# Inverses' transfers behind the queries' rotation, the substitution behind the keys', and modulation steps in the attention

## The chip, the core and the metric

The kernel runs on one core of a Trainium2 chip. The metric is the device time of one execution in microseconds (us); it is measured in several runs and the median is given. Engines: TensorE (PE), VectorE (DVE), ScalarE (ACT), GpSimd (POOL) and SyncE (SP), which here only issues DMAs.

## The reference

Two networks of two layers each follow one another on an activation x of 256 tokens by 1024 features, in float32.

A layer of the first is `x = norm(a*x + hybrid_mixer(x))`, then the same with a cross-attention to a memory, then with an MLP, `square(relu(x @ w_up)) @ w_down`. The hybrid mixer runs three attentions on one projection: a sparse one (compressed, selected and window branches), a latent one and one with forget gates.

A layer of the second is

```python
mod = c_act @ w_ada + b_ada                  # c_act = silu(c), 1024 x 3072
shift, scale, gate = split(mod)
h = rms_norm_2(x, norm_g) * (1.0 + scale) + shift
# h @ w_in is split into a pool branch, a retention (q, k, v, gate) and an RWKV-7 branch
qh = rotary(q); kh = rotary(k) * dh ** -0.5  # 4 heads of 128; rotate-half with cos, sin
# RWKV-7, for each token: S = S * w + (S a) b + v k;  y = S r
x = x + gate * (merged @ w_out)
```

The modulation `mod` depends on c alone, so its product with w_ada (24 pieces of 512 KB a layer) can be made anywhere ahead of the second network.

## The kernel before

**Products and weights.** Every float32 product is three TensorE products of split operands (`mm3`, L138 to L140). A weight unit of 512 KB is loaded by SP in program order (`fetch`) into one of four `raw` buffers; ACT casts it to `hi` (L112), DVE subtracts to get `lo` (L113); each has six slots. `gemm_b` makes a tile of 128 features by 256 tokens, `gemm_a` of 128 tokens by 512 features. A tile scheduler places the instructions of DVE, ACT and POOL; PE's order is written out by hand in the attention and in the second network.

**Side jobs.** `fillers` is a list of small jobs that `fill(n)` takes from. For each of the first network's layers it holds first a set-up job (`clear_scratch`, which writes zeros to two DRAM scratch arrays `zd` and `lt`, or the three `trig_steps` that make `cos` and `sin`), then the 24 modulation steps of one layer of the second network (`ada_steps`). A step loads a piece of w_ada into a `raw` buffer and lets DVE multiply it by c and reduce (L1641, one instruction and a read of the accumulator). `fill` is called in the MLP alone: one job after each pair of tiles of `up` for g of 1 and more (L929), and two, two and four jobs in `down` (L939); `fill(99)` empties the list at the end of the layer.

**Attention of the first network.** The loop at L730 goes through a list of slots. Each slot advances one or two of the jobs (m0, m1: latent; c0, c1: compressed; 00 to 11: selected and window; f0, f1: forgetting) and one piece of the dense products that run beside them (`dense`). The softmax steps are DVE's (L275 and on), the transposes go through one `t` buffer in PSUM, which DVE copies out (L315, L627 is a transpose of the compressed branch).

**Rotation and substitution in the second network.** RWKV-7's recurrence is solved in chunks, and the chunks' triangular matrices are inverted from blocks of 16. `masked` writes the matrices to the scratch `lt`, `band` reads their diagonal blocks back, and 15 rounds of a product and a sum on DVE (L1518, L1519: the substitution) invert all the blocks at once. The result goes through POOL's queue to `zd` (L1520), and four transfers, also on POOL's queue, read it back in another layout as `TT` (`inverse_parts`, L1195). `invert` (L1202) reads TT later. Beside it `rotated` (L1372 and on) makes the keys (chunk 4) and then the queries (chunk 3): four tiles each, and for each tile two ACT copies into a `row` buffer (three such buffers), a POOL product with sin (L1384), a DVE product with cos (L1386) and a POOL sum into `gt` (L1387). Behind the queries PE does the first half of a gate (`silu_gate`, two of four tiles), the retention's scores (L1398) and its state products (L1403).

## Time and profile before

| what | value |
|---|---|
| median of 3 runs | 1619.14 us (1618.19 to 1619.34) |
| the profiled execution's own time | 1620.32 us |
| its span in the profile | 1618.5 us |
| mean granted PE clock | 0.978 |
| PE busy | 1554.8 us, 96% |
| PE weight load busy | 1432.2 us, 88% |
| DVE, ACT, POOL busy | 1100.4, 744.8, 261.1 us |
| DMA moved | 288.98 MB, 179 GB/s on average |

Busy times are sums over an engine's instructions. The span is the profile's time from first to last instruction. A bracket behind a row of a timeline, `[2.79 <-POOL gt L1387]`, is the time that the engine stood idle before it, and whose result it waited for. The granted clock is 1.00 at 2.4 GHz and 0.50 at 1.2 GHz.

### The profile page before, as it was taken

The page shows a single profiled execution, that of the slowest core. Times are in us where ns is not written, and L with a number is a line of the kernel's source. Part 1 is how long each engine was busy: PE and PEld are TensorE (multiplying, and loading weights), DVE is VectorE, ACT ScalarE, POOL GpSimd, SP SyncE. Part 2 cuts the span into 40 slices and gives each one's busy share as a digit, 9 for nine tenths or more (in the row PEclk, how much of TensorE's full clock was granted, in tenths as well). Part 3 has the DMA queues.
Part 4 walks back from the last instruction along what each step waited for, and adds up shares of the span by engine and source line. Part 5 has one row for each costly group of instructions (what it writes and reads, how often), then busy time and mean ns, then how long its engine had stood idle before and what let it go on. Part 6 is the DMA issues. An engine that isn't in the chain of part 4 may idle for free. (4 is left out here: it accounts for less than half of the span.)

```text
span 1618.5 us, 29835 instructions
## 1 busy us (share of the span) xinstructions
PE 1554.8 (96%) x12106; PEld 1432.2 (88%) x12106; DVE 1100.4 (68%) x1785; ACT 744.8 (46%) x1196; POOL 261.1 (16%) x255
## 2 busy tenths in 40 slices
PE   7999999999999999999999899899999998999998
PEld 6789997999878899988988788899999987999997
DVE  5576568767676766689776787666466775764754
ACT  4665444544445664455543374433444643333441
POOL 1000110101100001201111142401111433201202
PEclk9899999999999999999999989999999999999999
DMA  8733475587776234664777744543355435442451
GB/s 296 257 105 119 158 231 172 179 287 264 266 258 204 89 108 154 204 208 141 253 270 252 265 140 161 162 147 120 102 183 161 155 113 168 163 134 90 154 184 67
DMA packets 81033, 288.98 MB, mean 179 GB/s; under 512 B 9224, under 2 KB 10304, under 8 KB 80896
## 3 DMA queue, kind: packets, MB, share of 16 engines
q1 hardware_dynamic: 78768, 280.07, 51.9%
q0 software_dynamic: 2128, 7.01, 1.5%
q8 instruction: 95, 1.56, 0.4%
q14 instruction: 42, 0.34, 0.1%
HBM read 281.48 MB, written 5.55 MB: 177 GB/s over the span
## 5 line engine op out<-in xcount | busy, mean ns | idle before, releaser
L113 DVE TENSOR_TENSOR lo<-raw,hi 128x1024 fp32r<-128x1024 f32 (+1 forms) x429 | 543.3, 1275 | 227.3 <-ACT hi L112 224.6
L112 ACT CAST hi<-raw 128x1024 fp32r<-128x1024 f32 (+1 forms) x435 | 452.7, 1048 | 508.8 <-PE mm L139 220.9
L138 PE MATMUL mm<-act,hi 128*128 128x256 f32 x1744 | 506.1, 290 | 7.8 <-ACT hi L112 5.8
L140 PE MATMUL mm<-act,lo 128*128 128x256 f32 x1744 | 497.7, 285 | 3.2 <-DVE lo L113 3.2
L139 PE MATMUL mm<-act,hi 128*128 128x256 f32 x1744 | 497.0, 285 | 0.5 <-DVE act L128 0.5
L138 PEld LDWEIGHTS mm<-act,hi 128*128 128x128 f32 x1744 | 336.8, 193 | 15.8 <-ACT hi L112 6.2
L140 PEld LDWEIGHTS mm<-act,lo 128*128 128x128 f32 x1744 | 336.4, 193 | 5.4 <-DVE lo L113 3.9
L139 PEld LDWEIGHTS mm<-act,hi 128*128 128x128 f32 x1744 | 336.6, 193 | 2.0 <-DVE act L128 0.9
L138 PE MATMUL s<-act,hi 128*128 128x256 f32 x448 | 128.5, 287 | 5.5 <-ACT PT L921 5.5
L138 PE MATMUL mm<-hi,act 128*128 128x512 f32 (+1 forms) x320 | 125.2, 392 | 6.5 <-ACT hi L127 5.5
L140 PE MATMUL s<-act,lo 128*128 128x256 f32 x448 | 128.2, 286 | 0.0
L139 PE MATMUL s<-act,hi 128*128 128x256 f32 x448 | 128.2, 286 | 0.0
L139 PE MATMUL mm<-lo,act 128*128 128x512 f32 (+1 forms) x320 | 123.4, 386 | 0.9 <-DVE lo L113 0.9
L140 PE MATMUL mm<-hi,act 128*128 128x512 f32 (+1 forms) x320 | 123.2, 385 | 0.0
L138 PEld LDWEIGHTS s<-act,hi 128*128 128x128 f32 x448 | 87.4, 195 | 6.4 <-ACT PT L921 6.1
L139 PEld LDWEIGHTS s<-act,hi 128*128 128x128 f32 x448 | 87.3, 195 | 0.2
L140 PEld LDWEIGHTS s<-act,lo 128*128 128x128 f32 x448 | 87.5, 195 | 0.0
L1641 DVE CUSTOM_DVE_ANT_0 raw<-raw,gt 128x1024 f32<-128x1024 f32 x48 | 59.5, 1239 | 30.6 <-DMA raw<-in_w_ada 30.3
L138 PEld LDWEIGHTS mm<-hi,act 128*128 128x128 f32 x320 | 61.1, 191 | 19.6 <-ACT hi L127 5.5
L926 POOL TENSOR_TENSOR PT<-PT 128x512 f32<-128x512 f32 x28 | 38.5, 1376 | 236.3 <-ACT act L925 128.4
L138 PE MATMUL mm<-hi,P 128*128 128x512 f32 x192 | 74.8, 389 | 0.0
L139 PE MATMUL mm<-lo,P 128*128 128x512 f32 x192 | 74.8, 389 | 0.0
(519 smaller groups left out, 2439.8 us busy)
## 6 DMA issues: line engine op xcount, KB each, us to landing
raw<-in_w_in SPq DMA_DIRECT2D x119, 512.0 KB, 4.4
raw<-in_w_up SPq DMA_DIRECT2D x64, 512.0 KB, 4.5
raw<-in_w_down SPq DMA_DIRECT2D x64, 512.0 KB, 4.7
raw<-in_w_gate SPq DMA_DIRECT2D x48, 512.0 KB, 3.4
raw<-in_w_ada SPq DMA_DIRECT2D x48, 512.0 KB, 4.5
raw<-in_w_gl SPq DMA_DIRECT2D x48, 512.0 KB, 3.8
raw<-in_w_branch SPq DMA_DIRECT2D x24, 512.0 KB, 3.4
raw<-in_w_br SPq DMA_DIRECT2D x16, 512.0 KB, 3.3
```

The lines of the kernel that those rows point to most:

```text
L112: act.copy(out=h[:, :cols], in_=r[:, :cols])
L113: (eng or ver).tensor_sub(out=l[:, :cols], in0=r[:, :cols], in1=h.bitcast(F32)[:, :cols])
L138: pe.matmul(o, lhsT=lh, rhs=rh, start=first, stop=False)
L139: pe.matmul(o, lhsT=lh, rhs=rl, start=False, stop=False)
L140: pe.matmul(o, lhsT=ll, rhs=rh, start=False, stop=last)
L926: pool.tensor_mul(out=r, in0=r, in1=r)
L1641: ver.tensor_tensor_reduce(out=r, in0=r, in1=box["c"], scale=1.0, scalar=0.0, op0=ALU.mult, op1=ALU.add, accum_out=mods[l][:, o:o + 1])
```

## The change

Three things are changed.

*Second network.* The four TT transfers keep their place in the program on POOL's queue, which is behind all of the queries' rotation; before, the scheduler was free to place them. The substitution, and the zd transfer with it, is issued behind the last cosine product of the keys (`issue_after(last[0])`).

*Modulation.* c's activation is made once and kept in a tile of its own (`cmod`), where it was made once a layer in a `gt` buffer. The first ten steps of a layer come ahead of the set-up jobs in the list, and in the attention's slot loop every second slot takes one job as soon as more than three attention jobs have begun. `down` takes one job where it took two or four.

*Tiles.* Two tiles change their tag, from `flat` to `mv`.

```diff
--- before.py
+++ after.py
@@ -456,7 +456,7 @@
         pool.memset(rep, 0.0)
 
         def compress_hidden(i):
-            fl = bt("flat", [128, 16, 2, 16])
+            fl = bt("mv", [128, 16, 2, 16])
             pool.memset(fl[:, :, :, 15:16], 0.0)
             for g in range(2):
                 for par in range(2):
@@ -727,6 +727,7 @@
             job = {"m": attend_mla, "f": attend_fox, "c": attend_compressed}
             jobs = {}
             pieces = dense()
+            beside = 0
             for slot in ("m0", "c0", "m1", "m0 c0", "m0 00", "m1 c1", "m1 01", "00 c1", "00 f0", "01 10", "01 10", "f0",
                          "f0 f1", "10", "10", "10 11", "11", "f1", "f1", "11", "11", "11"):
                 for n in slot.split():
@@ -734,6 +735,10 @@
                         jobs[n] = job[n[0]](int(n[1])) if n[0] in job else attend_nsa(int(n[0]), int(n[1]))
                     next(jobs[n], None)
                 next(pieces, None)
+                if len(jobs) > 3:
+                    beside += 1
+                    if beside % 2 and beside < 20:
+                        fill(1)
             for _ in pieces:
                 pass
         x = xs[0]
@@ -936,7 +941,7 @@
                 us = [unit(T["w_down"][l, 16 * c + 4 * g + i]) for i in range(4)]
                 gemm_a([ys[0][c], ys[1][c]], op, us, first=g == 0, last=g == 3, t_outer=g == 3 and c == 1)
                 if g < 3:
-                    fill(2 if g < 2 else 4)
+                    fill(1)
                     continue
                 if c == 1:
                     nrm.params(l, 2)
@@ -1192,7 +1197,8 @@
 
             for n in range(2):
                 for a in range(2):
-                    pool.dma_start(out=TT[n][half(a)], in_=flat(K["zd"], 16 + 8 * HS * n + 64 * 129 * a, [128, 64], [HS, 8], [1, 64]))
+                    tc.keep_in_program_order(pool.dma_start(
+                        out=TT[n][half(a)], in_=flat(K["zd"], 16 + 8 * HS * n + 64 * 129 * a, [128, 64], [HS, 8], [1, 64])))
 
         def invert():
 
@@ -1369,6 +1375,8 @@
                 act.activation(out=gv, in_=p, func=AF.Tanh, scale=0.5)
                 ver.scalar_tensor_tensor(out=gv, in0=gv, scalar=1.0, in1=p, op0=ALU.add, op1=ALU.mult)
 
+        last = []
+
         def rotated(c):
             us = chunk_b(c)
             dst = bt("gt", [128, 4, 256])
@@ -1383,7 +1391,7 @@
                     act.copy(out=sw[64:128], in_=pi[0:64, :])
                     pool.tensor_mul(out=sw, in0=sw, in1=sin)
                     dv = dst[:, j + i, :]
-                    ver.tensor_mul(out=dv, in0=pi, in1=cos)
+                    last[:] = [ver.tensor_mul(out=dv, in0=pi, in1=cos).ins]
                     pool.tensor_add(out=dv, in0=dv, in1=sw)
             return dst
 
@@ -1505,19 +1513,20 @@
             bonus()
             rk_ = rotated(4)
             pool.tensor_mul(out=Ei, in0=Ei, in1=rT)
-            zb = bt("PT", [128, 31, 16])
-            pool.memset(zb, 0.0)
-            pool.memset(zb[:, 15:31, 0:1], 1.0)
-            tmp = bt("dg", [128, 256])
-            zrow = zb[:, 15:31, :]
-            for i in range(14, -1, -1):
-                m = 15 - i
-                zv = bass.AP(tensor=zrow.tensor, offset=zrow.offset + 16 * i + 15 + 1,
-                             ap=[list(zrow.ap[0]), [1, m], [15, m]])
-                tv = tmp[:, :m * m].rearrange("p (a b) -> p a b", b=m)
-                ver.tensor_mul(out=tv, in0=zv, in1=band[:, i, 1:m + 1].unsqueeze(1).broadcast_to([128, m, m]))
-                ver.reduce_sum(out=zrow[:, i, 1:m + 1], in_=tv, axis=AX.X)
-            pool.dma_start(out=flat(K["zd"], 16, *blocks), in_=zrow)
+            with tc.issue_after(last[0]):
+                zb = bt("PT", [128, 31, 16])
+                pool.memset(zb, 0.0)
+                pool.memset(zb[:, 15:31, 0:1], 1.0)
+                tmp = bt("dg", [128, 256])
+                zrow = zb[:, 15:31, :]
+                for i in range(14, -1, -1):
+                    m = 15 - i
+                    zv = bass.AP(tensor=zrow.tensor, offset=zrow.offset + 16 * i + 15 + 1,
+                                 ap=[list(zrow.ap[0]), [1, m], [15, m]])
+                    tv = tmp[:, :m * m].rearrange("p (a b) -> p a b", b=m)
+                    ver.tensor_mul(out=tv, in0=zv, in1=band[:, i, 1:m + 1].unsqueeze(1).broadcast_to([128, m, m]))
+                    ver.reduce_sum(out=zrow[:, i, 1:m + 1], in_=tv, axis=AX.X)
+                pool.dma_start(out=flat(K["zd"], 16, *blocks), in_=zrow)
             rq = rotated(3)
             dm = aux(T["ret_decay"]).rearrange("p (h t) -> p h t", t=256)
             inverse_parts()
@@ -1625,15 +1634,16 @@
                                          op0=ALU.mult, op1=ALU.mult)
                 fetch(out[128 * t:128 * t + 128, s], o)
 
+    box = {}
+
     def ada_steps(l):
 
-        box = {}
 
         def step(j, i):
             def f():
                 if not box:
                     r = raw_load(T["c"].partition_broadcast(128))
-                    c = box["c"] = bt("gt", [128, 1024])
+                    c = box["c"] = bt("cmod", [128, 1024])
                     act.activation(out=c, in_=r, func=AF.Tanh, scale=0.5)
                     ver.scalar_tensor_tensor(out=c, in0=c, scalar=1.0, in1=r, op0=ALU.add, op1=ALU.mult)
                 r = raw_load(T["w_ada"][l, j, i])
@@ -1654,7 +1664,7 @@
     scratch = {n: dr.tile([128 * 2080], F32, name=n) for n in ("zd", "lt")}
 
     def clear_scratch():
-        z = bt("flat", [128, 16, 2, 16]).rearrange("p a b c -> p (a b c)")[:, 0:416]
+        z = bt("mv", [128, 16, 2, 16]).rearrange("p a b c -> p (a b c)")[:, 0:416]
         pool.memset(z, 0.0)
         for d in scratch.values():
             pool.dma_start(out=flat(d, 0, [2080, 128], [416, 5], [1, 416]),
@@ -1708,7 +1718,8 @@
         blk[:] = b1, s1
         xop = new_op(8)
         for l in range(L):
-            fillers.extend((trig_steps() if l == 1 else [clear_scratch]) + ada_steps(l))
+            steps = ada_steps(l)
+            fillers.extend(steps[:10] + (trig_steps() if l == 1 else [clear_scratch]) + steps[10:])
             x, xop, us = block1_layer(l, x, xop, us, K1)
     r = xop
     fill(99)
```

**POOL, second network, layer 0.** The end of the keys' rotation and the queries' rotation; L1384 and L1387 are the sine product and the sum, `zd` the scratch, TT the tiles for the inverses. Before:

```order
L1387 TENSOR_TENSOR gt_10482<-gt_10482,row_10599 128x256
L1520 DMA zd<-PT_10606 2048x1x16
L1195 DMA TT_10355<-zd 64x8x64
L1384 TENSOR_TENSOR row_10715<-row_10715,sin 128x256
L1195 DMA TT_10355<-zd 64x8x64
L1387 TENSOR_TENSOR gt_10665<-gt_10665,row_10715 128x256
L1384 TENSOR_TENSOR row_10721<-row_10721,sin 128x256
L1195 DMA TT_10356<-zd 64x8x64
L1387 TENSOR_TENSOR gt_10665<-gt_10665,row_10721 128x256
L1195 DMA TT_10356<-zd 64x8x64
L1384 TENSOR_TENSOR row_10776<-row_10776,sin 128x256
L1387 TENSOR_TENSOR gt_10665<-gt_10665,row_10776 128x256
```

In the changed kernel the same lines are L1392, L1395, L1529 (zd) and L1200 (TT):

```order
L1395 TENSOR_TENSOR gt_10660<-gt_10660,row_10710 128x256
L1392 TENSOR_TENSOR row_10716<-row_10716,sin 128x256
L1395 TENSOR_TENSOR gt_10660<-gt_10660,row_10716 128x256
L1529 DMA zd<-PT_10601 2048x1x16
L1392 TENSOR_TENSOR row_10771<-row_10771,sin 128x256
L1395 TENSOR_TENSOR gt_10660<-gt_10660,row_10771 128x256
L1392 TENSOR_TENSOR row_10777<-row_10777,sin 128x256
L1395 TENSOR_TENSOR gt_10660<-gt_10660,row_10777 128x256
L1200 DMA TT_10350<-zd 64x8x64 x2
L1200 DMA TT_10351<-zd 64x8x64 x2
```

The zd transfer moved behind the queries' second sum, and all four TT transfers behind their fourth.

**DVE, at the same place.** L1518 and L1519 are the substitution's product and sum, L1386 the cosine product, L113 the weights' `lo` (`lo_10656` and `lo_10662` belong to the queries' weights, `lo_10798` is the first of the gate's). Before:

```order
L113 TENSOR_TENSOR lo_10656<-raw_10653,hi_10655 128x1024
L1518 TENSOR_TENSOR dg_10609<-PT_10606,dg_10353 128x49
L1519 TENSOR_REDUCE PT_10606<-dg_10609 128x7
L113 TENSOR_TENSOR lo_10662<-raw_10659,hi_10661 128x1024
L1386 TENSOR_TENSOR gt_10482<-mm_10483,cos 128x256
L1518 TENSOR_TENSOR dg_10609<-PT_10606,dg_10353 128x64
L1519 TENSOR_REDUCE PT_10606<-dg_10609 128x8
...
L1386 TENSOR_TENSOR gt_10482<-mm_10544,cos 128x256
L1519 TENSOR_REDUCE PT_10606<-dg_10609 128x15
L1386 TENSOR_TENSOR gt_10665<-mm_10666,cos 128x256 x2
L113 TENSOR_TENSOR lo_10798<-raw_10795,hi_10797 128x1024
```

In the changed kernel (L1527 and L1528 the substitution, L1394 the cosine product; `lo_10793` the first of the gate's):

```order
L113 TENSOR_TENSOR lo_10657<-raw_10654,hi_10656 128x1024
L1394 TENSOR_TENSOR gt_10477<-mm_10478,cos 128x256 x2
L1394 TENSOR_TENSOR gt_10477<-mm_10539,cos 128x256 x2
L1527 TENSOR_TENSOR dg_10604<-PT_10601,dg_10348 128x1
L1528 TENSOR_REDUCE PT_10601<-dg_10604 128x1
...
L1527 TENSOR_TENSOR dg_10604<-PT_10601,dg_10348 128x225
L1528 TENSOR_REDUCE PT_10601<-dg_10604 128x15
L113 TENSOR_TENSOR lo_10793<-raw_10790,hi_10792 128x1024
L1394 TENSOR_TENSOR gt_10660<-mm_10722,cos 128x256
L113 TENSOR_TENSOR lo_10799<-raw_10796,hi_10798 128x1024
```

The keys' four cosine products stand ahead of the whole substitution, and the gate's first `lo` directly behind its last sum.

**DVE, attention of layer 0**, the third modulation step of nine; L286 to L290 scale the softmax's rows, L315 copies a transpose out of `t`, L613 begins the compressed branch. Before:

```order
L286 RECIPROCAL sc_1085<-sums_873 128x4
L288 TENSOR_TENSOR sc_1085<-sc_1085,gate_631 128x4
L290 TENSOR_TENSOR P_871<-P_871,sc_1085 128x4x128
L315 COPY PT_962<-t_957 128x512
L613 TENSOR_TENSOR pcs_971<-s_972,bias_c 128x4x2x16
L286 RECIPROCAL sc_1089<-sums_874 128x4
```

In the changed kernel (the step is the two rows L1651):

```order
L286 RECIPROCAL sc_1096<-sums_873 128x4
L1651 ISA raw_1236,mod_76<-raw_1236,cmod_956 128x1024
L1651 ISA mod_76 128x1
L315 COPY PT_970<-t_965 128x512
L613 TENSOR_TENSOR pcs_979<-s_980,bias_c 128x4x2x16
L288 TENSOR_TENSOR sc_1096<-sc_1096,gate_631 128x4
L286 RECIPROCAL sc_1100<-sums_874 128x4
```

The step stands between the reciprocal and the copy of the transposes.

## Rows read from the trace of the kernel before

**Rows 1.** The page's first part: engine, busy us, share of the span, instructions.
```profile
PE 1554.8 (96%) x12106; PEld 1432.2 (88%) x12106; DVE 1100.4 (68%) x1785; ACT 744.8 (46%) x1196; POOL 261.1 (16%) x255
```

**Rows 2.** Busy time by window: stretch, length, five engines, granted clock, DMA share, GB/s.
```profile
60.00:180.00 120.00, 117.91 (x970) 107.11 (x970) 78.07 (x202) 74.57 (x178) 3.22 (x6) 1.00 0.40 134
300.00:525.00 225.00, 221.39 (x1449) 199.71 (x1448) 159.40 (x202) 109.26 (x147) 22.72 (x20) 0.99 0.77 257
760.00:921.00 161.00, 156.69 (x965) 141.46 (x964) 115.12 (x146) 76.78 (x88) 18.48 (x14) 0.99 0.78 263
1020.00:1052.00 32.00, 26.13 (x185) 24.68 (x184) 19.42 (x27) 12.23 (x19) 14.73 (x17) 0.89 0.46 127
1344.00:1384.00 40.00, 32.26 (x244) 31.40 (x244) 27.25 (x52) 15.23 (x26) 19.25 (x21) 0.87 0.46 141
```

**Rows 3.** Timeline of PE, block 2 layer 0: start, us, instruction, idle before and releaser.
```profile
1032.09 0.38 PE L138 MATMUL mm<-act,hi 128*128 128x256 f32 x1 [0.55 <-ACT hi L112]
...
1037.53 1.03 PE L1398 MATMUL mm<-gt,gt 128*128 128x256 f32 x4
1041.34 0.70 PE L1398 MATMUL mm<-gt,gt 128*128 128x256 f32 x2 [2.79 <-POOL gt L1387]
1043.82 1.22 PE L1398 MATMUL mm<-gt,gt 128*128 128x256 f32 x2 [1.77 <-POOL gt L1387]
```

**Rows 4.** Timeline of POOL, the same place.
```profile
1025.38 1.12 POOL L1520 DMA_DIRECT2D zd<-PT  x1
1032.80 0.71 POOL L1195 DMA_DIRECT2D TT<-zd  x1 [6.30 <-DMA zd<-PT]
```

**Rows 5.** Timeline of PE, block 2 layer 1.
```profile
1367.49 0.39 PE L140 MATMUL mm<-act,lo 128*128 128x256 f32 x1 [0.59 <-DVE lo L113]
...
1374.21 0.58 PE L138 MATMUL mm<-act,hi 128*128 128x256 f32 x1 [5.28 <-ACT hi L112]
...
1376.89 0.58 PE L140 MATMUL mm<-act,lo 128*128 128x256 f32 x1 [1.88 <-DVE lo L113]
...
1382.60 1.68 PE L1398 MATMUL mm<-gt,gt 128*128 128x256 f32 x7
```

**Rows 6.** Timeline of ACT, the same place.
```profile
1372.35 0.37 ACT L1382 COPY row<-mm 64x256 f32<-64x256 f32 x1 [6.17 <-POOL gt L1387]
```

**Rows 7.** Groups by line on DVE, whole kernel: count, busy us, mean ns, idle before.
```profile
L1518 DVE TENSOR_TENSOR dg<-PT,dg 128x1 f32<-128x1 f32 (+14 forms) x30 | 10.6, 352 | 3.6 <-DMA dg<-lt 2.8
...
L1519 DVE TENSOR_REDUCE PT<-dg 128x1 f32<-128x1 f32 (+14 forms) x30 | 7.1, 237 | 0.8
...
L1386 DVE TENSOR_TENSOR gt<-mm,cos 128x256 f32<-128x256 f32 x16 | 6.7, 419 | 15.5 <-ACT row L1383 15.5
```

**Rows 8.** The page's fifth part: two groups of DVE.
```profile
L113 DVE TENSOR_TENSOR lo<-raw,hi 128x1024 fp32r<-128x1024 f32 (+1 forms) x429 | 543.3, 1275 | 227.3 <-ACT hi L112 224.6
...
L1641 DVE CUSTOM_DVE_ANT_0 raw<-raw,gt 128x1024 f32<-128x1024 f32 x48 | 59.5, 1239 | 30.6 <-DMA raw<-in_w_ada 30.3
```

**Rows 9.** Busy time by window, three short stretches (columns as in rows 2).
```profile
421.00:426.00 5.00, 5.00 (x32) 5.00 (x31) 3.23 (x4) 2.51 (x4) 2.60 (x2) 0.66 0.48 166
828.00:830.00 2.00, 2.00 (x11) 2.00 (x11) 0.69 (x1) 1.78 (x2) 0.56 (x1) 0.50 0.91 330
1370.00:1380.00 10.00, 3.91 (x16) 3.62 (x17) 6.23 (x5) 5.45 (x8) 9.81 (x12) 0.51 0.45 138
```

**Rows 10.** Timeline of PE, the MLPs of layers 0 and 1.
```profile
419.90 0.39 PE L138 MATMUL s<-act,hi 128*128 128x256 f32 x1 [2.39 <-ACT PT L921]
...
826.84 0.39 PE L138 MATMUL s<-act,hi 128*128 128x256 f32 x1 [1.77 <-ACT PT L921]
```

**Rows 11.** Timeline of PE, the attention of layer 0.
```profile
107.90 0.33 PE L627 MATMUL t<-cpack,pcs 128*128 128x128 f32 x1 [1.19 <-DVE PT L315]
```

**Rows 12.** Timeline of POOL, block 2 layer 1.
```profile
1374.32 0.74 POOL L1387 TENSOR_TENSOR gt<-gt,row 128x256 f32<-128x256 f32 x1
...
1375.82 1.61 POOL L1387 TENSOR_TENSOR gt<-gt,row 128x256 f32<-128x256 f32 x1
```

## The prediction

> **What bounds the kernel now.** I read the engines' busy shares first. PE is busy for 1554.8 of 1618.5 us [rows 1], so the span is PE's work plus about 64 us in which it stands still, plus what the lower clock costs. An edit that touches none of PE's own matmuls can only win or lose there. So the table by stage comes next [rows 2]: its last three columns are PE's granted clock, the DMA share and the rate. Three kinds of place matter. In the attention of layer 0 PE loses 2.09 us of 120 (first row), with the DMA at 0.40, and layer 1 runs the same program. In the two MLPs it loses 3.61 and 4.31 us, with the DMA at 0.77 and 0.78. Around the keys' and queries' rotation of block 2 it loses 5.87 of 32 us and 7.74 of 40 us, and the clock falls to a mean of 0.89 and 0.87. Then I read the timelines there.
>
> In layer 0 of block 2 PE has finished the first half of the gate at 1037.5, does four score matmuls and waits 2.79 and 1.77 us for POOL's `gt` add [rows 3]. POOL is late because it issues the zd transfer at 1025.38 and then sits 6.30 us on its landing in front of the first TT transfer [rows 4]; the queries' sine products stand behind that TT. In layer 1 the same wait reaches PE another way: PE waits 0.59, 5.28 and 1.88 us in the gate [rows 5], since ACT's copy into `row` waited 6.17 us for POOL's add [rows 6] and the gate's casts stand behind that copy on ACT.
>
> **Part 1: TT and substitution in block 2.** After the change all four TTs stand behind the last query add on POOL, and the substitution stands behind the keys' last cosine product on DVE. Nothing new reads TT early: its readers, the inverses' transposes, stand over a hundred PE instructions behind the scores. So POOL's 6.30 us goes. What is late next is the gate's weights: their `lo` subtractions now stand behind the whole substitution on DVE.
>
> How long is that? A gate or rotation matmul costs 0.12 us (117.91 us for 970 [rows 2]). The gate of layer 0 starts about 12 matmuls ahead of 1032.09 less its 0.55 us wait [rows 3], near 1030.0; the queries' 96 matmuls take 11.5 us, so PE leaves the keys at 1018.5. Four ACT copies of 0.37 [rows 6] and two products of 0.42 [rows 7] later, at 1020.8, the substitution starts. It is 30 instructions, 10.6 and 7.1 us for both layers, so 8.9 us a layer [rows 7]; two cosine products of the queries (0.8) stand inside it, and I allow 1 us for the gaps between 30 dependent instructions, a tenth of their time, for which no row here stands: 10.7 us, to 1031.5. One subtraction of 1.28 [rows 8] later, at 1032.8, the gate's third matmul may go, which PE wanted at 1030.2: **a new wait of 2.6 us**. The second unit's subtraction, behind another product, adds 0.3; 34 more matmuls take 4.1, and the scores start at 1038.6, 1.1 later than before, but with their operands there. Gone are 2.79 + 1.77 = 4.6 us. The mean clock of 0.89 over 32 us is some 7 us at the half level; 4.6 of these were the waits, the other 2.4 us were matmuls that took twice their time (1.2 saved inside the window, about as much just after it). Layer 0: 4.6 + 2.4 - 1.1 = 5.9 us won.
>
> Layer 1: the gate's third matmul was wanted near 1366.8 (1367.49 less its wait of 0.59 [rows 5]). By the same steps the keys end at 1355.1, the substitution runs from 1357.4 to 1368.1, and the subtraction is done at 1369.4: again 2.6 us of wait. The scores start at 1369.4 + 1.2 + 0.3 + 4.1 = 1375.0 in place of 1382.60 [rows 5]: 7.6 us won. Together **13.5 us**.
>
> What can be given back is the clock. A wait of 2.39 us in the MLP was followed by a granted clock of 0.66 over 5 us, one of 1.77 us by the 1.2 GHz level (0.50) for the 2 us looked at [rows 9, 10]; the attention's wait of 1.19 us [rows 11] stands in a stage with a mean of 1.00 [rows 2]. Two new gaps of 2.6 us lie above both that fell. 5 us at 0.66 lose 1.7 us, so I take **3.4 us back** for the two: 10.1 us. Bounds: no new wait and no fall would win both windows' idle and slow time, 5.87 + 7.74 + 2.4 + 2 = 18 us (1370 to 1380 stood at 0.51 with 3.91 us busy, some 2 us too many [rows 9]); a substitution of twice my gaps and a clock that stays low as long as in layer 1 leave about 5.
>
> One cost speaks against the new order: POOL's products of the queries now run beside DVE's subtractions for the gate. Such a pairing shows before: a POOL add that takes 0.74 us takes 1.61 [rows 12]. Four at 1.61 behind a zd issue of 1.12 [rows 4] end at 1039.1, when the second half of the scores wants them, so I book nothing for it, and up to 1 us a layer in the range. The Trainium skill, page "SBUF — State Buffer", section "SBUF: two separate sides", says that VectorE and GpSimd hold a shared port pair as an exclusive lock, also when VectorE has two SBUF inputs. By that rule the substitution's products, with two SBUF inputs, would wait for POOL's rotation too, and the sum would be about 1 us a layer worse, by an estimate from the doubled add. The doubled add agrees with it; that the substitution is slowed, no row here settles.
>
> **Part 2: modulation steps.** A step is a 512 KB load into one of four `raw` buffers, a DVE product-and-reduce of 1.24 us [rows 8] and a short read. Ten come first in the list, the order shows nine a layer in the attention. They leave `down`; those in `up` stay.
>
> MLP, what it wins: both windows lose 3.61 + 4.31 us in waits [rows 2], and 1.7 and 1 us of slow matmuls behind the two waits named [rows 9, 10]: 10.6 us at most. DVE waits 30.6 us for the steps' loads in all [rows 8], so relief is plausible, but 15 of 24 steps stay, among them all that stand between `up`'s weights. I take 9/24 of 10.6: **4 us**; ends 0 and 10.6. The estimate is coarse: if the one late chain of 2.39 us goes with its slow matmuls, that is 4 us at once.
>
> Attention, what it costs: nine steps are 9 x 1.24 = 11 us of DVE a layer, on top of 78.07 busy in 120 [rows 2]; DVE has the room, but its softmax chain ends some waits of PE last, the `t` transpose at 107.90 among them [rows 11]. Ends: 0, if each step falls in DVE's idle time, and 2 x 11 = 22 us, if each lies on the path. PE's lost 2.09 us sit in few places, so I take two steps in nine as falling ahead of what PE waits for, 2.5 us a layer: **5 us lost**. On SP's queue the steps' loads stand ahead of later weights of the attention, which then wait for one more buffer; with the DMA at 0.40 [rows 2] I count that as 0. ACT gets c's activation there, whose table is the one that the softmax behind it needs: 0, beside ACT's idle third.
>
> **Part 3: the rest.** c is loaded, activated and multiplied once and not twice, which takes a cast-sized ACT and a DVE instruction off layer 1's MLP: 0, beside PE's work. The clear's two transfers leave the start of the kernel for layer 0's MLP, on POOL's queue in front of nothing that PE waits for: 0; without that cover, a few us at worst.
>
> **Sum.** -10.1 - 4 + 5 = -9.1. The profiled execution took 1620.32 us (span 1618.5), 1.2 above the runs' median of 1619.14; against the median the forecast is **1610.0 us**.
>
> **Rivals.**
> *The wait moves and little is left.* The gate's `lo` behind the substitution is later than I say, the clock falls at each gap and stays low as in layer 1 (0.51 for 10 us [rows 9]); block 2 wins 5, the MLP nothing: -5 + 5 = 0, about 1619; with half the attention's cost, 1616. For it: the new gap is as long as any outside block 2. Against: 5.28 us of layer 1's wait has no successor of that size.
> *Slower: the attention's chain on DVE decides.* From eleven or twelve of the eighteen steps on that lie ahead of what PE waits for, 14.1 / 1.24, the loss eats what block 2 and the MLP win; with all of them, 22 - 14 = +8, 1627, and more with the clock. For it: the softmax steps feed PE through `s` and `t` buffers that are few. Against: DVE is idle for a third of the stage.
> *Larger gain.* The gaps leave the clock up and the MLP's late chain goes whole: -13.5 - 10 + 3 = -20, about 1599.
> *The change doesn't do what it says in the MLP.* The steps that hurt are those in `up`, which stay: -10.1 + 5 = -5, 1614.
>
> **How the numbers follow.** Forecast case (1605 to 1613) 0.43; larger gain (1596 to 1605) 0.17; MLP unchanged (1613 to 1616) 0.19; little left (about 1616 to 1622) 0.09; slower by the attention 0.12. A measurement of this kernel tells a change from none at about 0.2%, 3.2 us. So faster 0.79, same 0.09, slower 0.12. The range is 1600 to 1618: it leaves out the slower case, part of the same, and the far end of the gain, about 0.2.
>
> **What would show it.** In block 2: no POOL idle before a TT; a PE wait on `lo` at the gate of 2 to 3 us a layer in place of the `gt` and `hi` waits; scores 5 to 8 us earlier after the stage's start; the clock at the half level or not behind the gap. In the MLP windows: idle below 3.6 and 4.3 us. In the attention windows: PE idle up by 1 to 5 us each, behind `t` or `s`. It is wrong if the attentions lose more than 10 us in all, or if the gate's wait exceeds 5 us.

## The result and the profile after

The changed kernel takes 1603.03 us (median of 4 runs, 1601.58 to 1606.92) beside 1619.24 us for the kernel before (1618.19 to 1622.14). The ratio is 0.9907, with an interval of 0.9883 to 0.9931: 11 to 19 us less. The forecast was 1610.0, in a range of 1600 to 1618. The profiled execution of the changed kernel is the longest of its four, 1606.92 us with a span of 1605.1.

The page's first part, against [rows 1]:

```profile
PE 1548.5 (96%) x12106; PEld 1427.4 (89%) x12106; DVE 1094.4 (68%) x1784; ACT 741.7 (46%) x1193; POOL 259.5 (16%) x255
```

PE is busy 6 us less, in a span that is 13 us shorter: slow matmuls went as well as waits. The same three windows as in [rows 2] (stretch, length, the five engines' busy time, granted clock, DMA share, GB/s):

```profile
60.00:180.00 120.00, 116.98 (x949) 104.98 (x948) 87.83 (x221) 74.63 (x179) 3.23 (x6) 0.99 0.51 169
300.00:525.00 225.00, 223.62 (x1473) 201.87 (x1471) 151.50 (x189) 111.80 (x148) 23.15 (x20) 1.00 0.73 243
760.00:921.00 161.00, 160.64 (x998) 145.31 (x997) 111.81 (x142) 75.97 (x92) 22.04 (x18) 1.00 0.71 239
```

The attention of layer 0 has 9.8 us more of DVE work (nine steps of 1.24 us are 11), and PE stands still for 3.02 us where it did for 2.09. The MLPs, which lost 3.61 and 4.31 us, lose 1.38 and 0.36, and their DMA share fell from 0.77 and 0.78 to 0.73 and 0.71. The whole list of PE's waits, three of its rows (engine, line, what was waited for: us in total, times, longest):

```profile
PE mm L140 <- DVE lo L113: 5.8, 2, 3.0
PE mm L138 <- DVE kT L1376: 4.9, 2, 3.8
...
PE t L627 <- DVE PT L315: 2.7, 2, 1.3
```

All four waits of the first two rows stand in block 2. The second row is new; the first had three shorter waits before, 3.2 us in all. The 5.5 us behind `PT L921`, the MLP's, are gone, and of POOL's `gt` nothing is left.

All 12106 matmuls stand in both traces, almost all in the same order, so each can be compared with itself. Counted by the same matmul at the stages' edges, the 13 us of the profiled execution are made of:

| stage | forecast | changed kernel | its second profile | block2_only | steps_only | tt_late | steps_tt_late |
|---|---|---|---|---|---|---|---|
| start, to 56 us | 0 | +1.4 | -0.5 | 0.0 | -0.7 | -1.3 | -0.9 |
| attention and cross-attention, layer 0 | +2.5 | +2.6 | +1.9 | +0.3 | +2.7 | +0.2 | +2.1 |
| entry to the MLP, layer 0 | 0 | +1.0 | +1.0 | 0.0 | +1.0 | 0.0 | +1.0 |
| MLP, layer 0 | -4 for both | -4.2 | -4.2 | +0.4 | -4.2 | +0.7 | -4.2 |
| attention and cross-attention, layer 1 | +2.5 | +0.5 | -1.5 | -0.2 | +0.3 | -0.3 | -1.3 |
| MLP, layer 1, to block 2 | see above | -9.1 | -9.6 | -0.4 | -9.1 | -1.1 | -9.6 |
| block 2 to the rotation, layer 0 | 0 | +1.2 | +3.6 | -0.1 | +1.2 | +0.2 | +1.0 |
| rotation to the inversion, layer 0 | -4.2 | +0.8 | +1.4 | -2.1 | -1.3 | -7.0 | -6.1 |
| on to layer 1's rotation | 0 | -2.5 | +0.1 | -1.4 | -1.4 | -2.4 | 0.0 |
| rotation to the inversion, layer 1 | -5.9 | -4.4 | -3.5 | -3.9 | -0.9 | -6.7 | -6.7 |
| the rest | 0 | 0.0 | -3.1 | -1.5 | -1.6 | -3.1 | -3.1 |

(Differences against the one profile of before, in us; the experiments are told below.) Rows that should be zero show how much of such a difference is chance: -3.1 to +3.6, mostly where a stretch at the half clock stands in one trace and not in the other. Each column is one execution; those of tt_late and steps_tt_late are 6 and 2 us faster than the median of their runs. What is larger, or the same in all columns that share a part, is the change: the MLPs won 13 us, not 4; the rotation in layer 0 of block 2 won nothing.

Why it did not is in the timelines. PE in layer 0, to hold against [rows 3]:

```profile
1025.82 0.54 PE L140 MATMUL mm<-act,lo 128*128 128x256 f32 x1 [2.78 <-DVE lo L113]
...
1032.93 1.89 PE L1406 MATMUL mm<-gt,gt 128*128 128x256 f32 x8
...
1048.67 0.47 PE L138 MATMUL mm<-hi,act 128*128 128x512 f32 x1 [3.82 <-DVE kT L1376]
```

and in layer 1, against [rows 5]:

```profile
1360.85 0.58 PE L140 MATMUL mm<-act,lo 128*128 128x256 f32 x1 [3.03 <-DVE lo L113]
...
1367.76 1.89 PE L1406 MATMUL mm<-gt,gt 128*128 128x256 f32 x8
```

In both layers the waits for `gt` and `hi` became one wait for the gate's `lo`, of 2.78 and 3.03 us; the eight scores follow without a break. But in layer 0 PE then waits 3.82 us for `kT`, in a product behind the second half of the gate. ACT shows why:

```profile
1039.59 1.05 ACT L112 CAST hi<-raw 128x1024 fp32r<-128x1024 f32 x1 [1.82 <-DMA raw<-in_w_in]
1043.94 1.05 ACT L112 CAST hi<-raw 128x1024 fp32r<-128x1024 f32 x1 [3.30 <-DMA raw<-in_w_in]
...
1047.21 0.59 ACT L1375 ACTIVATE kT<-mm 128x512 f32<-128x512 f32 x1
```

The weights' casts wait for their loads, 1.82 and 3.30 us, and the gate's activation (L1375), which `kT` needs, stands behind them. The load that the second of these casts waits for is issued at 1034.29 and takes 9.55 us to land. POOL, against [rows 4], no longer waits for zd's landing ahead of the queries' products, and TT comes last. It still has one wait among them: 2.03 us for the end of the substitution, before it issues zd.

```profile
1024.92 1.13 POOL L1529 DMA_DIRECT2D zd<-PT  x1 [2.03 <-DVE PT L1528]
...
1026.90 1.60 POOL L1395 TENSOR_TENSOR gt<-gt,row 128x256 f32<-128x256 f32 x1
...
1030.26 1.60 POOL L1395 TENSOR_TENSOR gt<-gt,row 128x256 f32<-128x256 f32 x1
1032.87 2.77 POOL L1200 DMA_DIRECT2D TT<-zd  x4 [1.00 <-DMA zd<-PT]
```

### The profile page after: what moved, and what is told of

Same layout as the page of the kernel before. It is cut to its first block, busy times and chain, and to the rows that moved or that the text cites. A ratio compares the mean times of both kernels' runs of the same rounds, so it can differ in the third digit from the quotient of the medians.

```text
span 1605.1 us, 29832 instructions
## 1 busy us (share of the span) xinstructions
PE 1548.5 (96%) x12106; PEld 1427.4 (89%) x12106; DVE 1094.4 (68%) x1784; ACT 741.7 (46%) x1193; POOL 259.5 (16%) x255
## 4 chain that ended last, share of the span: by engine, by line
PE 78%; DVE 11%; ACT 3%; DMA 3%; issue 3%; POOL 1%; SPq 0%; DVEq 0%; POOLq 0%; ACTq 0%
PE mm L138 19%; PE mm L139 18%; PE mm L140 18%; DVE lo L113 3%; PE s L140 3%; PE s L139 3%; PE s L138 3%; DMA raw<-in_w_in 2%; ACT hi L112 2%; PE s L270 1%; PE s L1173 1%; PE o L657 1%; PE o L1276 1%; DVE dg L1527 1%; PE t L1276 1%
## 5 line engine op out<-in xcount | busy, mean ns | idle before, releaser
L113 DVE TENSOR_TENSOR lo<-raw,hi 128x1024 fp32r<-128x1024 f32 (+1 forms) x429 | 540.6, 1270 | 230.3 <-ACT hi L112 227.6
L1651 DVE CUSTOM_DVE_ANT_0 raw<-raw,cmod 128x1024 f32<-128x1024 f32 x48 | 61.2, 1276 | 33.6 <-DMA raw<-in_w_ada 33.2
L138 PE MATMUL mm<-hi,P 128*128 128x512 f32 x192 | 74.8, 389 | 0.0
L140 PE MATMUL mm<-hi,P 128*128 128x512 f32 x192 | 74.7, 389 | 0.0
```

Of the source, the lines that this page charges most:

```text
L113: (eng or ver).tensor_sub(out=l[:, :cols], in0=r[:, :cols], in1=h.bitcast(F32)[:, :cols])
L138: pe.matmul(o, lhsT=lh, rhs=rh, start=first, stop=False)
L140: pe.matmul(o, lhsT=ll, rhs=rh, start=False, stop=last)
L1651: ver.tensor_tensor_reduce(out=r, in0=r, in1=box["c"], scale=1.0, scalar=0.0, op0=ALU.mult, op1=ALU.add, accum_out=mods[l][:, o:o + 1])
```

## Experiments

Two theories stood at first. *A*, read from the trace of the changed kernel: the steps' move carries most of the gain, and in block 2 the late substitution costs what the pinned transfers win. *B*, the forecast's split: block 2 ten, the steps about nothing. The kernel before took 1619.6, 1615.8 and 1615.3 us beside the three groups of runs, so groups are compared by their ratios to it.

**block2_only**: the kernel before with the second network's part of the change alone.

```diff
+                    tc.keep_in_program_order(pool.dma_start(out=TT[n][half(a)], ...
+            with tc.issue_after(last[0]):      # around zb, the 15 rounds and the zd transfer
```

> Only the second network's part: TT kept in program order, substitution behind the keys' last cosine product; the modulation steps stand as before. Theory A (read from the changed kernel's trace): this part is worth about 5 us, all in layer 1, because in layer 0 a new wait of 3.8 us behind the gate's product gives it all back: 1614, 1611 to 1616. Theory B (the forecast's split): 10 us, 5.9 less half of the clock's cost in layer 0 and the rest in layer 1: 1609, 1607 to 1611.

Measured: 1611.31 us (12 runs), ratio 0.9964, 0.9944 to 0.9985, so 2 to 9 us won. PE's waits around the rotation of layer 0:

```profile
PE mm L140 <- DVE lo L113: 3.0, 1, 3.0
PE mm L138 <- DVE kT L1371: 1.4, 1, 1.4
```

The interval holds A's 5 us and not B's 10. The wait behind the gate's product is there in layer 0 too, with 1.4 us, so the stage still won 2.1, where A had nothing.

**steps_only**: all of the change but the second network's part.

> Only the modulation: nine steps a layer in the attention, c once in its own tile, one job in down, clear_scratch later; the second network as before. Theory A: 12 us won in the MLPs (3 in layer 0, 9 in layer 1), 2 to 3 lost in layer 0's attention: 1609, 1607 to 1611. Theory B: 4 won and 5 lost: 1620, 1617 to 1622.

Measured: 1606.22 us (6 runs), ratio 0.9918, 0.9898 to 0.9937: 10 to 17 us won. A's size, and B falls. The MLPs' windows are those of the changed kernel, and in block 2 the old waits stand:

```profile
300.00:525.00 225.00, 223.13 (x1472) 201.36 (x1471) 150.42 (x190) 112.13 (x152) 22.95 (x20) 1.00 0.74 242
760.00:921.00 161.00, 158.53 (x981) 143.24 (x979) 111.90 (x145) 76.08 (x92) 22.51 (x18) 1.00 0.71 236
```

```profile
PE mm L1403 <- POOL gt L1392: 4.3, 2, 2.5
```

(The idle 2.5 us of the second window are the start of the wait behind the norm at the MLP's end, which before stood outside the window.) The two parts sum to 0.0118 of the time, the changed kernel has 0.0093 with an interval of 0.0069 to 0.0117: together they give no more than their sum, and perhaps less.

**tt_late**: the kernel before, only that the four TT transfers are issued behind the queries' last sum.

```diff
+                    last[:] = [pool.tensor_add(out=dv, in0=dv, in1=sw).ins]
+            with tc.issue_after(last[0]):
+                inverse_parts()
```

In the programs as built this gives, instruction for instruction on all five engines, the same order as the change's `keep_in_program_order` on the TT transfers alone; so it is also the change without its substitution part and without its steps.

> Kernel before with the four TT transfers issued behind the queries' last sum on POOL, substitution left where it was. Theory A: the POOL wait is all of the loss and the substitution ahead of the gate's lo is pure cost, so the 13.6 us of waits in the two windows go and most of the slow matmuls behind them: 1604, 1602 to 1608. Rival C: the substitution in front of the keys' cosine products holds the queries just as long, and little more than in block2_only comes: 1609 to 1614.

Measured: 1605.41 us (6 runs), ratio 0.9899, 0.9876 to 0.9923: 12 to 20 us. POOL and PE's waits in layer 0:

```profile
1024.10 1.12 POOL L1522 DMA_DIRECT2D zd<-PT  x1
1025.21 0.78 POOL L1386 TENSOR_TENSOR row<-row,sin 128x256 f32<-128x256 f32 x1
...
1032.44 1.60 POOL L1389 TENSOR_TENSOR gt<-gt,row 128x256 f32<-128x256 f32 x1
1033.99 2.77 POOL L1195 DMA_DIRECT2D TT<-zd  x4
```

```profile
PE mm L140 <- DVE lo L113: 1.1, 1, 1.1
PE mm L138 <- ACT hi L112: 0.5, 1, 0.5
```

POOL doesn't wait for zd, the queries' sums end at 1034, and PE loses 1.6 us where it lost 5.87. A holds, C falls: with the substitution's rounds among the keys' products POOL waits once 2.44 us for a cosine product, but PE loses nothing by it. This alone wins more than twice what block2_only does (0.0101 of the time against 0.0036, in the same group of runs), by moving less: issuing the substitution late is a cost.

**steps_tt_late**: both together, the change without `issue_after(last[0])`.

> steps_only and tt_late together. Theory A: the two gains add, 10 + 14: 1595, 1592 to 1599, faster than the changed kernel by about 8. Rival C: no faster than the changed kernel, 1602 to 1606.

Measured: 1594.39 us (4 runs), ratio 0.9843, 0.9818 to 0.9868: 21 to 29 us under the kernel before. The gains add within the noise (0.0082 and 0.0101 for the parts, 0.0157 together), and it beats the changed kernel: by about 9 us by the medians, by 10 to 14 by the ratios (0.9843 against 0.9907 and 0.9928).

**after_again**: the changed kernel once more.

> The changed kernel once more. Theory A (with the substitution behind the keys, the gate's four units hold all four raw buffers and the weight stream stops for some 10 us, and what follows depends on how fast the stream recovers): 12 to 16 us under the kernel before; the DMA share between the two halves of the rotation near 0 in both layers; the wait of 3.8 us behind the gate's product may or may not be there. Rival G: that wait is fixed, and so it shows again, 3 us or more.

Measured: 1603.7 us (6 runs), ratio 0.9928, 0.9911 to 0.9945. The wait behind the gate's product came back with 4.2 us, so in layer 0 of this kernel it is nearly fixed in size, as rival G has it. It isn't so elsewhere: layer 1 has 1.1 and 2.0 us in the two profiles, and block2_only 1.4 in both layers. The stop of the weight stream that A names is there. The busy time by window, in each layer first from the keys to the end of the substitution, then behind it:

```profile
1008.00:1024.00 16.00, 12.90 (x107) 12.57 (x105) 13.04 (x38) 6.50 (x14) 9.49 (x13) 0.98 0.12 41
1024.00:1046.00 22.00, 18.72 (x137) 18.04 (x137) 14.10 (x16) 10.00 (x12) 8.55 (x9) 0.94 0.96 244
1348.00:1361.00 13.00, 10.68 (x90) 10.48 (x88) 11.21 (x35) 5.04 (x10) 5.69 (x8) 1.00 0.00 1
1361.00:1383.00 22.00, 19.29 (x139) 18.58 (x140) 15.72 (x24) 10.02 (x12) 10.45 (x9) 0.92 0.94 246
```

The same two stretches in steps_tt_late:

```profile
1008.00:1024.00 16.00, 14.32 (x117) 13.91 (x117) 11.12 (x19) 8.71 (x15) 12.48 (x14) 1.00 0.32 77
1024.00:1046.00 22.00, 21.06 (x139) 19.13 (x139) 15.75 (x36) 8.44 (x9) 4.42 (x6) 1.00 0.80 230
1337.00:1350.00 13.00, 11.97 (x98) 11.56 (x97) 9.15 (x17) 6.27 (x14) 8.34 (x10) 1.00 0.32 91
1350.00:1372.00 22.00, 20.40 (x149) 19.05 (x150) 17.48 (x32) 10.54 (x14) 12.21 (x12) 1.00 0.84 262
```

With the substitution in front of the gate's `lo`, the DMA share is 0.12 and 0.00 in the first stretch: the gate's four units have landed, all four `raw` buffers are held until DVE's subtractions, and SP cannot issue the next load. In the second stretch everything is wanted at once, at shares of 0.96 and 0.94. In steps_tt_late the shares are 0.32 in the first stretches and 0.80 and 0.84 in the second. The stop itself is not new. From one issue of a `raw` load to the next, the longest stop at the rotation is 12.0 us in layer 0 and 9.4 in layer 1 of the kernel before, and 11.5 to 12.4 and 9.3 to 9.5 in every run without the late substitution. In the four traces with it (block2_only, the changed kernel twice, after_nopin) it is 16.0 to 16.8 and 18.2 us. How long PE then waits doesn't follow from the length of the stop alone: layer 1 has the longer stop and the shorter wait.

**after_nopin**: the changed kernel with the scheduler free to place TT.

```diff
-                    tc.keep_in_program_order(pool.dma_start(
-                        out=TT[n][half(a)], ...
+                    pool.dma_start(out=TT[n][half(a)], ...
```

> The changed kernel with the scheduler free to place the TT transfers: with the substitution late, the first stands ahead of the queries' third sum on POOL and waits there for zd. Theory A: the scores wait some 2 to 4 us a layer for the queries' sums, so 4 to 8 us slower than after_again. Rival H: with the substitution late the place of TT costs nothing, within 2 us of after_again.

Measured: 1605.09 us (6 runs), ratio 0.9944, 0.9929 to 0.9959, against 0.9928 for after_again: not told apart, which is nearer to H. PE's waits around the rotation of layer 1:

```profile
PE mm L1405 <- POOL gt L1394: 3.2, 2, 1.9
```

The mechanism of A is there, 3.2 us for the queries' sums in layer 1 (and 2.4 in layer 0). But the 4.2 us behind the gate's product were not there in layer 0: one wait took the other's place. Why is argued, not shown: the later scores gave the weight stream time. That the TT transfers, all at once in the changed kernel, slow the loads beside them is not borne out: here they are issued from 1031.33 to 1037 with sums between them, and the loads still land in 6.7 us at the median, for 6.9 in the changed kernel.

Four runs then asked what it is in the MLP that the steps cost. *A*, the place: steps in `down` delay the next weights of `up`. *D*, the number: the weight stream as a whole is too much with 24 steps.

**down_only** and **up_only**, both from steps_tt_late: 15 steps a layer, all in `down`; and all 24 in `up`, none in `down` or the attention.

```diff
-                    if g:
-                        fill(1)
...
-                    fill(1)
+                    fill(2 if g < 2 else 4)
```

```diff
-                if len(jobs) > 3:
-                    beside += 1
-                    if beside % 2 and beside < 20:
-                        fill(1)
...
-                        fill(1)
+                        fill(2)
...
-                    fill(1)
                     continue
```

> steps_tt_late, but the 15 steps that are left in a layer's MLP all stand in down (two, two and four jobs, as before) and none in up. Theory A (the place decides: each PE wait in the MLP begins with steps that down puts between its own weights and those of the next up): the MLPs' waits come back, 8 to 12 us: 1604, 1601 to 1607. Rival D (the number decides, 15 steps in place of 24): no change against steps_tt_late, 1592 to 1597.

> steps_tt_late, but without steps in the attention and without any in down: up takes two jobs where it took one, all 24 of a layer. Theory A: the MLPs stay free of waits and the attention's 2 us come back: 1592, 1590 to 1595. Rival D (the number decides): most of the 12 us that the MLPs won are lost, 1602 to 1607.

Measured: down_only 1598.08 us, ratio 0.9888 (0.9861 to 0.9915); up_only 1602.22 us, ratio 0.9916 (0.9888 to 0.9944), both 6 runs. MLP windows of down_only, then of up_only:

```profile
300.00:515.00 215.00, 213.22 (x1424) 193.90 (x1424) 142.72 (x170) 103.79 (x131) 20.75 (x20) 1.00 0.74 245
...
750.00:905.00 155.00, 155.00 (x1004) 142.22 (x1004) 107.38 (x135) 77.36 (x90) 19.30 (x15) 1.00 0.73 238
```

```profile
300.00:515.00 215.00, 211.23 (x1402) 190.95 (x1401) 153.99 (x188) 102.15 (x129) 25.98 (x19) 1.00 0.78 264
...
750.00:905.00 155.00, 149.86 (x969) 137.80 (x968) 115.45 (x146) 74.14 (x88) 19.73 (x15) 0.99 0.79 262
```

By its time down_only fits neither theory well: its ratio is 0.0045 above that of steps_tt_late, 7 us, where A had 8 to 12 and D none, and its interval just overlaps. The traces decide. With 15 steps the MLPs stay free of waits for weights wherever these stand, so A falls. down_only's MLPs cost 1 us more each than those of steps_tt_late, at their end; in layer 0 that is the wait behind the norm, 1.7 us for 0.8, with steps in front of the norm on DVE. Most of the rest of its extra time is stretches at the half clock. With 24 the waits are back though no step stands in `down`: 3.8 and 5.1 us idle, at 264 and 262 GB/s. Of the 3.8 us, 1.9 are for weights; 0.8 behind the norm stand in the kernel before too.

**c_once**: the kernel before with c made once and the two tiles' tag changed.

> Kernel before with c's vector made once in a tile of its own, and the two tiles' tag changed; no step moves. Theory A: two table loads, an activation and a DVE instruction fewer in layer 1's MLP are worth 0 to 2 us: 1618, 1616 to 1620. Rival E: they are the larger part of what layer 1's MLP won, 1611 to 1614.

Measured: 1615.30 us (12 runs), ratio 0.9995, 0.9976 to 1.0014. No difference; E falls.

**clear_first**: steps_tt_late with the clear as the attention's first job.

```diff
-            fillers.extend(steps[:10] + (trig_steps() if l == 1 else [clear_scratch]) + steps[10:])
+            fillers.extend(steps[:10] + trig_steps() + steps[10:] if l == 1 else [clear_scratch] + steps)
```

> steps_tt_late, with layer 0's clear of the two scratch arrays as the first job in the attention in place of the eleventh, behind the cross-attention; nine jobs there are then the clear and eight steps. Theory A: the wait of 1.4 us at the MLP's first transposes of layer 0 is due to the clear's place and goes, and one step fewer delays the attention: 1593, 1591 to 1595. Rival F: the wait comes from another cause and stays, 1594 to 1597.

Measured: 1592.69 us (5 runs), ratio 0.9847, 0.9823 to 0.9871: not told apart from steps_tt_late's 0.9843. In its trace the wait of 1.4 us in front of the MLP's first transposes of layer 0 is gone, and the entry to the MLP costs 0.0 in place of 1.0 us; so the clear's place was its cause, and it is too small for the clock of the runs to show.

**att_18** and **att_5**: steps_tt_late with 18, and with five or six, steps a layer in the attention.

```diff
-                    if beside % 2 and beside < 20:
-                        fill(1)
+                    fill(1)
...
-            fillers.extend(steps[:10] + (trig_steps() if l == 1 else [clear_scratch]) + steps[10:])
+            fillers.extend(steps[:18] + (trig_steps() if l == 1 else [clear_scratch]) + steps[18:])
```

```diff
-                    if beside % 2 and beside < 20:
+                    if beside % 4 == 1:
...
-                    fill(1)
+                    fill(1 if g else 2)
```

> steps_tt_late with a step in every slot of the attention from the fifth on, 18 a layer in place of nine; six a layer are left to the MLP. Theory A: the MLPs have nothing left to win, and the further nine steps cost the attention at least what the first nine did in layer 0, 2 to 8 us in all: 1597 to 1603 on a chip where steps_tt_late takes 1594 to 1595. Rival I: DVE has room for them, no change within 2 us.

> steps_tt_late with five or six steps a layer in the attention in place of nine, two jobs instead of one in down for g = 0; 18 or 19 are left to the MLP. Rival D as the runs now read (the MLP's weight stream on the DMA queue decides, and it runs dry when the steps' loads are too many): the first waits come back, 2 to 6 us: 1597 to 1601. The other reading (half of the relief is enough): within 2 us of steps_tt_late, 1593 to 1597.

Measured: att_18 1597.75 us, ratio 0.9891 (0.9873 to 0.9909); att_5 1595.01 us, ratio 0.9876 (0.9858 to 0.9895), 4 runs each. att_18's attention of layer 0, by window and by PE's waits:

```profile
60.00:180.00 120.00, 116.92 (x947) 104.66 (x946) 96.63 (x241) 73.54 (x178) 3.24 (x6) 0.99 0.61 211
```

```profile
PE s L824 <- DVE P L816: 1.7, 1, 1.7
PE t L627 <- DVE PT L315: 1.5, 1, 1.5
```

DVE is busy 96.63 of 120 us and PE still loses only 3.08: by the same matmul the attention costs 3.4 us against 2.1 with nine steps. Its interval stands above that of steps_tt_late, by about 8 us at the middle. But the two belong to different groups of runs, and the changed kernel itself came out at 0.9907 and 0.9928 in two groups, so some 3 of the 8 us can be that. 1.3 us are the attention of layer 0, and most of the rest is stretches at the half clock that its trace has and the other has not, which I can't tie to the steps. In its own group its interval overlaps that of att_5, which has a third of the steps there. So A's direction is that of the traces, and its size is not shown. att_5's interval overlaps that of steps_tt_late. att_5's MLPs:

```profile
300.00:515.00 215.00, 214.10 (x1431) 194.42 (x1429) 150.10 (x188) 104.09 (x134) 22.34 (x20) 1.00 0.77 255
...
750.00:905.00 155.00, 155.00 (x988) 141.50 (x987) 113.85 (x140) 76.61 (x89) 17.39 (x14) 1.00 0.77 256
```

No wait in layer 1 and 0.9 us in layer 0, behind the norm at the MLP's end, where the kernel before has 0.8 too, at 255 and 256 GB/s: half the relief was enough, and the waits that D expected did not come.

## Why the prediction came out as it did

The direction was right, and the time lies in the range. The sum was not: 16 us were won by the medians, 11 to 19 by the interval, for a forecast of 9.1. Two of its terms were off by much and in opposite directions, block 2 (2 to 4 us won at the two rotations for a forecast of 10.1) and the MLPs (13 for 4), and that the time still fell into the range is luck. 1603.03 us lies in the case "larger gain" (1596 to 1605), which had a chance of 0.17; of its two conditions, the MLPs' came and the clock's did not.

**Block 2, the new wait.** "A new wait of 2.6 us" at the gate was measured at 2.78 and 3.03. The clock did what was said: both gaps were followed by slow matmuls, the eight scores start 9.9 us after the gate's third matmul was wanted (1032.93 less 1025.82 - 2.78), where I had 8.4 in layer 0 and 8.2 in layer 1, so 1.5 and 1.7 us of each went to the clock as forecast. The substitution took 10.9 us in layer 0 (1013.73 to 1024.63) for 10.7. Layer 1 won 3.5 to 4.4 us for a forecast of 5.9.

**Block 2, the step that failed** is "What is late next is the gate's weights", taken as all that is late. I followed the delay of the `lo` subtractions to PE and not to the buffers that they free. SP's queue stood behind these, and the loads of the next weights with it; the price, 3.8 and 4.2 us in layer 0, took all that the stage had won there: +0.8 and +1.4 in place of -4.2. That the late substitution costs more than it wins is shown by tt_late and steps_tt_late, which leave it out; the way from the longer stop to that wait is read from the traces. The rival "the wait moves and little is left" had this outcome for block 2, with another cause.

**The MLPs, the term that was mis-sized.** I took 9/24 of the 10.6 us that could be won. The steps' relief is not proportional: 13 us went with nine steps moved, and the same with five (att_5). The end was also too low, because a wait of 1.8 us behind the norm at the end of layer 1's MLP lay outside my window; and each wait that went took a slow stretch with it. That the steps in `up` would keep the waits alive, the reason of the rival for 1614, fell in down_only and up_only: the number of steps decides. DVE's 30.6 us of idle for their loads [rows 8], from which I argued, is no sign of it: it is 33.6 us in the changed kernel. How a step reaches PE can be read ahead of the wait of 2.39 us in the kernel before [rows 10]:

```profile
410.46 1.23 DVE L1641 CUSTOM_DVE_ANT_0 raw<-raw,gt 128x1024 f32<-128x1024 f32 x1 [2.95 <-DMA raw<-in_w_ada]
...
416.48 1.05 ACT L112 CAST hi<-raw 128x1024 fp32r<-128x1024 f32 x1 [5.12 <-DMA raw<-in_w_down]
```

The first load of the `down` weights is issued at 411.72, when the step's product has freed its `raw` buffer, and lands 4.66 us later. ACT's cast waits for it, and the copy (L921) that PE waits for stands behind the cast. It is block 2's mechanism again, a buffer held in front of the load queue. Whether a step hurts by holding the buffer, by its bytes or by DVE's 1.24 us, no run separates.

**The attentions.** 5 us forecast, 1.9 to 2.7 measured in layer 0 and nothing beyond chance in layer 1. The bound by DVE did not come even at 96.63 of 120 us.

**Part 3.** c once: 0, as said. The clear: 1.0 us, where I had 0 with "a few us at worst".

**The shared port.** POOL's sums beside the gate's subtractions take 1.60 us (1026.90, 1030.26), as was said from [rows 12]. The rule of the Trainium skill, page "SBUF — State Buffer", section "SBUF: two separate sides", that a VectorE instruction with two SBUF inputs and a GpSimd instruction that reads SBUF exclude each other for a whole instruction, shows in the substitution too:

```profile
1013.73 0.67 DVE L1527 TENSOR_TENSOR dg<-PT,dg 128x1 f32<-128x1 f32 x1
...
1014.62 0.59 DVE L1527 TENSOR_TENSOR dg<-PT,dg 128x4 f32<-128x4 f32 x1
...
1015.44 0.17 DVE L1527 TENSOR_TENSOR dg<-PT,dg 128x9 f32<-128x9 f32 x1
```

The first two products stand beside POOL's last sum and sine of the keys and take 0.67 and 0.59 us; the third, with more elements, takes 0.17. The trace agrees with the rule there. Its price was 0.3 to 0.5 us for each such product, three in layer 0 and four in layer 1: 1.4 and 1.7 us. The kernel before already paid 0.9 and 0.6 us in the same way, so the new order added 0.5 and 1 us, near the 1 us a layer of the estimate.

**Readings of the forecast that were wrong.** Of the 7 us at the half level in layer 0, 4.6 were not waits. The granted clock is 1.00 to 1042 us and 0.63 from 1042 to 1044, so the waits share at most 1.8 us with it, and some 5 us of matmuls ran at half speed; the 2.4 us that this gave back came out near that by chance. The sum to 1038.6 leaves out the second subtraction's 1.2 us, which the sum for layer 1 has. And the new gap was not as long as any outside block 2: the kernel before has waits of 3.3 (`t L471`) and 3.0 us (`t L357`) there.

## What to carry to other kernels

When work is put in front of a weight's last reader, follow the delay through the buffer to the load queue: a stage that holds all its input buffers stops the stream, and pays when it catches up. Pinning the four transfers alone was worth more than twice the two moves together, so try the parts of a change alone. And where a weight stream has few buffers, don't book relief by its share: in these MLPs five or six loads less of 24 took the waits away, and further ones brought nothing.

## What the runs showed of the hardware

In these two stages, with four buffers, little lies between waits and none. The MLPs showed no waits at 255 and 256 GB/s in 215 and 155 us windows with 18 or 19 steps (but 0.9 us behind the norm in layer 0), and 3.8 and 5.1 us of idle at 264 and 262 with 24; before, 3.6 and 4.3 at 257 and 263, in slightly longer windows [rows 2].

When the stream is released all at once, each transfer is slow. In the changed kernel from 1024 to 1046 us (output and input, queue, count, KB each, median us to landing):

```profile
raw<-in_w_in SPq DMA_DIRECT2D x8, 512.0 KB, 6.9
TT<-zd POOLq DMA_DIRECT2D x4, 128.0 KB, 7.8
```

Before, in the same stretch, the five weight loads took 4.2 us and the four TT transfers 3.4. In tt_late, with TT late and the shorter stop, they took 4.8 and 5.9 there, so part of it is TT's own bunching. And the granted clock differs between executions of one program: two profiles of the changed kernel differ by up to 3 us in stages that the change doesn't touch, so a stage's gain of 1 us can be read from one profile only where the same wait is in every one.
